# A float32 encoder block on one core: side work re-laned, operand parts made earlier, more weight halves kept

## The chip, the cores and the metric

The kernel runs on one NeuronCore of a Trainium2 chip. The metric is the device time of one execution in microseconds; the core's five engines (TensorE or PE, VectorE or DVE, ScalarE or ACT, GpSimd or POOL, SyncE or SP) run their own instruction streams in order and meet through semaphores. GpSimd does almost nothing here. Nearly all DMAs are issued from SP's queue, a few from ScalarE's.

## The reference

One layer (DEPTH is 1) on x of 2048 frames by 1024 channels, float32:

```
h = rmsnorm(x); proj = h @ w_in            # 1024 -> 512 | 2*512 | 1024 | 1024
u_pool, u_glu, g_a, g_b = split(proj)
A = pool_mixer(u_pool)      # 4 groups of 128: trailing mean over 2/4/8/16 frames minus self,
                            # times pool_w[g], times pool_scale, then @ w_pool_out (512 -> 1024)
B = conformer_conv(u_glu)   # a*sigmoid(gate); causal depthwise conv, 31 taps; layernorm; silu;
                            # then @ w_conv_out (512 -> 1024)
merged = sigmoid(g_a) * A + sigmoid(g_b) * B
x = x + rmsnorm(merged @ w_o)              # 1024 -> 1024
h = rmsnorm(x)
x = x + rmsnorm(square(relu(h @ w_up)) @ w_down)   # 1024 -> 4096 -> 1024
```

## The kernel before

Arithmetic. Every float32 operand is split into a high and a low part (`split`, L194; `split_w` for weights, L201): ScalarE casts the high part, VectorE subtracts it from the source to get the low one, and a product is three matmuls (high by high, high by low, low by high). On top of that the big projections use a scheme of seven block products in place of eight: an `Octet` (L365) runs products 1 to 7 on sums and differences of weight blocks (`weight_parts`, L258) and of token blocks (`token_parts`, L318). One product is 24 matmuls of 128x512. Operands are tiles of 128 x 1024.

Blocks and stages. The 2048 frames are two blocks of 1024. For each block: input projection (1 pool octet, 2 GLU octets, 2 octets for each gate: 49 products), branch A (`branch_a`, L901, 8 products), merge with branch B (`merge`, L922, 8 products), output projection (`out_proj`, L948, 8 products of 48 matmuls), up-projection (`mlp_up`, L1029, 8 octets, 56 products). The order on TensorE is: input 0, A 0, input 1, B 0, wo 0, A 1, up 0, B 1, wo 1, up 1, then the down-projection of both blocks in four slabs of 28 products (`down_product`, L1345), the last slab block by block, with the last norm behind it. Intermediate tensors (gates, convolution results `yd`, normed results `zd`, pooled results `mxd`, hidden activations `fd`) go through DRAM.

Side work. Convolution (`conv_steps`, L724: 31 VectorE operations per group of 128 channels, line 746), the layer norm and silu behind it (`norm_steps`, L761) and the pooling (`pool_steps`, L822, with four small products "mix") are generators. A `Lane` (L1074) advances its generators by a rate, and `bg` (L1103) calls every lane once after each product; `yield n` makes a lane sit out n calls. `behind` (L146) ties what they issue behind the instructions already issued for the main line, so that each engine's order is set when the program is built; `high_priority(offset=...)` moves what is issued within it that many instructions ahead. Weight loads and splits stand 260 ahead (`AHEAD`), 45 in the first stage.

In block 1's input projection one lane holds the rest of block 0's convolution, then `norm_steps(0, 1)`, then `pool_steps(1)`; what is left of it is issued after the last product by `empty` (L1112). Block 1's convolution runs in lanes beside B 0, wo 0 (rate 6, stopped after six calls) and up 0 (1.2, then 2.5), its norm behind it in up 0.

Weights. In block 0 the low halves of the input projection's weights, and for some octets the block sums, are written to DRAM (`kept`, through `flush`, L310, one product later) and loaded again in block 1. `load_w` (L213, for A, B and wo) splits each weight anew at every use. `out_proj` of block 0 runs both halves of the tokens (t = 0 and 1) under one weight, and that of block 1 one half after the other.

Parts. `Parts` (L350) makes an operand pair per step: for up 0 in branch A of block 1 (three steps of the norm's chain, then five parts), for up 1 only when up 1 begins.

Pools, in tiles of 128 x 1024: raw weights `wr` 5, weight sums `ws` 2, high and low weight halves 3 each, `big` 28 for operands, `tr` 8 for passing results, PSUM 3 accumulators.

Of the kernel before, what the change touches and what calls it, by code (L numbers as in the profile page):

```python
# [15 lines left out]
P = 128  # L16
# [3 lines left out]
TB = 1024  # L20
# [45 lines left out]
def block_kernel(  # L66
# [22 lines left out]
    p_wr = pool("pwr", 5)  # L89
# [76 lines left out]
    mean_c = p_const.tile([P, P], F32R, tag="meanc", name="mean_c")  # L166
    nc.gpsimd.memset(f32(mean_c), 1.0 / CW)
# [88 lines left out]
    kept = {}  # L256

    def weight_parts(src, key, b, keep, raw):  # L258
# [15 lines left out]
        def source(i):  # L274
            if i in (1, 2, 4):
                return get({1: 0, 2: 1, 4: 3}[i])
            if (key, i, "sum") in kept and b:
                t = mk(p_wr, "wr")
                load(t, kept[key, i, "sum"])
                return t  # L280
# [27 lines left out]
    later, due = [], []  # L308

    def flush():  # L310

        while due:
            load(*due.pop())
        due.extend(later)
        later.clear()
# [34 lines left out]
    class Parts:  # L350
# [8 lines left out]

        def need(self, i):  # L360
# [4 lines left out]
    class Octet:  # L365
# [13 lines left out]
        def run(self, i, then, bg):  # L379
# [11 lines left out]
            elif i == 2:  # L391
                self.sink(0, 0, ps, self.s1)
# [12 lines left out]
    def run_octets(octets, bg):  # L405
# [3 lines left out]
        for n, (o, i) in enumerate(jobs):  # L409
            o.run(i, jobs[n + 1][1] if n + 1 < len(jobs) else None, bg)  # L410
# [127 lines left out]
    p_tr = pool("ptr", 8)  # L538
# [97 lines left out]
    def in_stats(b):  # L636

        r = mk(p_ss, "r")
        for t in (0, 1):
# [13 lines left out]
            yield from inv_rms_steps([ss], inv_d, TR, 3, got)  # L653
# [70 lines left out]
    def conv_steps(b, groups):  # L724
# [8 lines left out]
        for c in groups:  # L733
# [5 lines left out]
            for k in range(TAPS):  # L739
# [9 lines left out]
                if k == 15 and c != groups[-1]:  # L749
                    nv = get(c + 1)  # L750
# [10 lines left out]
    def norm_steps(b, lag):  # L761
# [3 lines left out]
        mu = mk(p_y, "y")  # L765
        y = {}

        def prefetch(c):
            y[c] = window()
            load(y[c], yd[b, c, 0])  # L770

        for t in (0, 1):
            s = slice(t * T, (t + 1) * T)
            rb = mk(ps_rb, "rb", F32, (P, T))
            nc.tensor.matmul(rb, mean_c, sh[:, s], start=True, stop=False)
            nc.tensor.matmul(rb, mean_c, sl[:, s], start=False, stop=True)
            nc.scalar.copy(mu[:, s], rb)
            prefetch(t)
        yield 1
        ss = mk(p_ss, "sm")  # L780
        sq = {}
        for c in range(CC):
            sub(y[c], y[c], mu)
            load(yd[b, c, 0], y[c])
            sq[c] = ss if c == 0 else tr()
            nc.scalar.activation(sq[c], y[c], AF.Square)
            if c + 2 < CC:
                prefetch(c + 2)
            if c > 1:
                add(ss, ss, sq[c - 1])  # L790
            yield 1
        add(ss, ss, sq[CC - 1])
        yield lag
        r = mk(p_ss, "r")
        halves = [ss[:, t * T : (t + 1) * T] for t in (0, 1)]

        def got(t, rb):
            nc.scalar.copy(r[:, t * T : (t + 1) * T], rb)
            prefetch(t)

        yield from inv_rms_steps(halves, inv_c, TR, lag, got)
        yield 1
        hl = {}
        for c in range(CC + 1):
            if c < CC:
                mul(y[c], y[c], r)
                sg, ln = tr(), tr()
                nc.scalar.activation(sg, y[c], AF.Sigmoid, scale=col(C_LG + c), bias=col(C_LB + c))
                nc.scalar.activation(ln, y[c], AF.Identity, scale=col(C_LG + c), bias=col(C_LB + c))
                if c + 2 < CC:  # L810
                    prefetch(c + 2)
            if c:
                for i, part in enumerate(hl):
                    load(zd[b, c - 1, i], f32(part))
                yield
            if c < CC:
                yield 1
                mul(ln, ln, sg)
                hl = split(ln, *TR)
                yield  # L820

    def pool_steps(b):  # L822

        pw = []
# [9 lines left out]
        for g in range(CC):  # L834
            w, m = WINDOWS[g], 1
            while m < w:
                lo = HALO - (w - 2 * m)
                s2 = window(W)
# [13 lines left out]
            if not pw:  # L852
# [720 lines left out]
```

## Time and profile before

| what | value |
|---|---|
| median of 3 runs | 2504.81 us (2504.07 to 2507.45) |
| the profiled execution | 2504.89 us, of which its span is 2503.1 us |
| PE busy | 2254.7 us (90% of the span) |
| DVE busy | 1724.4 us (69%) |
| ACT busy | 1025.4 us (41%) |
| DMA | 538.93 MB, mean 215 GB/s |
| mean granted TensorE clock | 0.946 |

Busy time is the time in which an engine has an instruction in work; for matmuls, which are pipelined, a busy engine can still run at a lower granted clock, and the profile lists that clock by stretch. In rows of groups or of a timeline, the name ahead of the arrow is what is written, the names behind it what is read, `x` the count; in brackets stands the idle time before the first of them and what released it. In rows by stretch the columns are length, busy time and count of each engine, granted clock, busy share of the DMA engines, and GB/s.

### The profile page before, as it was taken

What the parts mean: (1) busy time and instruction counts of PE and PEld (TensorE: products, weight loads), DVE (VectorE), ACT (ScalarE), POOL (GpSimd) and SP (SyncE); (2) the same over time, 40 slices, a digit from 0 to 9 for tenths busy, and PEclk for the clock granted to TensorE, in tenths of its full rate; (3) what the DMA queues carried; (4) which work ended last, traced back from release to release, by engine and by line L of the source; (5) the groups of instructions that cost most, each with busy time, mean ns of one, the idle gap of its engine ahead of it and who ended that gap; (6) DMA issues with size and microseconds to landing.
All of it is one profiled execution on the core that took longest, in us unless ns stands there. A gap on an engine that the chain in (4) does not pass through costs nothing.

```text
span 2503.1 us, 24957 instructions
## 1 busy us (share of the span) xinstructions
PE 2254.7 (90%) x9600; PEld 1832.9 (73%) x9600; DVE 1724.4 (69%) x1685; ACT 1025.4 (41%) x1066; POOL 1.1 (0%) x11
## 2 busy tenths in 40 slices
PE   6898999999779987999869878999899999999885
PEld 5687877788667765888747656888678888787663
DVE  6797778883477497998653686767534566559676
ACT  5333443335422244445523464555344322223452
POOL 0000000000000000000000000000000000000000
PEclk9999999999889998999979888999899999999896
DMA  5667997657981562335583445786655454546774
GB/s 189 243 235 252 338 372 260 228 208 285 341 330 59 201 222 82 135 140 179 201 295 101 162 150 189 256 299 255 231 180 187 168 193 176 177 160 235 269 269 159
DMA packets 151320, 538.93 MB, mean 215 GB/s; under 512 B 17825, under 2 KB 17953, under 8 KB 151201
## 3 DMA queue, kind: packets, MB, share of 16 engines
q1 hardware_dynamic: 138528, 491.20, 55.0%
q10 hardware_dynamic: 12672, 46.14, 4.8%
q8 instruction: 75, 1.23, 0.2%
q14 instruction: 45, 0.36, 0.0%
HBM read 359.45 MB, written 177.83 MB: 215 GB/s over the span
## 4 chain that ended last, share of the span: by engine, by line
PE 79%; DVE 9%; DMA 6%; ACT 2%; issue 2%; SPq 1%; DVEq 0%; ACTq 0%
PE up L228 23%; PE down L228 23%; PE wo L228 7%; PE glu L228 6%; PE ga L228 6%; PE gb L228 4%; PE A L228 4%; PE B L228 3%; PE pool L228 2%; DMA tr<-fd 2%; DVE tr L119 2%; DVE y L746 1%; DVE tr L116 1%; DVE big L119 1%; DVE wl L119 1%
## 5 line engine op out<-in xcount | busy, mean ns | idle before, releaser
L228 PE MATMUL up<-big,wh 128*128 128x512 f32 x1792 | 497.8, 399 | 60.1 <-DVE tr L116 21.0
L228 PEld LDWEIGHTS up<-big,wh 128*128 128x128 f32 x1792 | 343.9, 193 | 140.8 <-ACT big L197 39.6
L228 PE MATMUL down<-fo,wh 128*128 128x512 f32 x896 | 359.1, 401 | 31.0 <-ACT fo L1340 31.0
L228 PE MATMUL down<-tr,wh 128*128 128x512 f32 x896 | 359.3, 401 | 15.3 <-DVE tr L119 15.3
L204 ACT CAST wh<-wr 128x1024 fp32r<-128x1024 f32 x170 | 177.8, 1048 | 473.7 <-PE up L228 106.6
L746 DVE SCALAR_TENSOR_TENSOR y<-v,cst,y 128x1024 f32<-128x1024 f32 x240 | 307.7, 1282 | 4.9
L228 PE MATMUL down<-fo,wl 128*128 128x512 f32 x896 | 284.1, 399 | 0.0
L228 PE MATMUL up<-big,wl 128*128 128x512 f32 x896 | 282.2, 397 | 0.0
L204 ACT CAST wh<-ws 128x1024 fp32r<-128x1024 f32 x124 | 130.6, 1053 | 323.9 <-PE up L228 138.8
L119 DVE TENSOR_TENSOR wl<-wr,wh 128x1024 fp32r<-128x1024 f32 x129 | 156.3, 1212 | 111.5 <-ACT wh L204 110.3
L228 PEld LDWEIGHTS down<-fo,wh 128*128 128x128 f32 x896 | 173.5, 194 | 73.7 <-ACT fo L1340 37.6
L228 PEld LDWEIGHTS down<-tr,wh 128*128 128x128 f32 x896 | 173.4, 194 | 58.9 <-DVE tr L119 22.9
L228 PEld LDWEIGHTS down<-fo,wl 128*128 128x128 f32 x896 | 173.1, 193 | 36.2
L228 PEld LDWEIGHTS up<-big,wl 128*128 128x128 f32 x896 | 172.7, 193 | 36.7
L1340 ACT CAST fo<-tr 128x1024 fp32r<-128x1024 f32 x112 | 117.5, 1050 | 197.1 <-DMA tr<-fd 104.9
L119 DVE TENSOR_TENSOR tr<-tr,fo 128x1024 fp32r<-128x1024 f32 x112 | 136.8, 1222 | 82.7 <-ACT fo L1340 82.7
L116 DVE TENSOR_TENSOR big<-big,down 128x1024 f32<-128x1024 f32 x88 | 107.1, 1219 | 125.6 <-PE down L228 122.7
L119 DVE TENSOR_TENSOR wl<-ws,wh 128x1024 fp32r<-128x1024 f32 x116 | 141.5, 1220 | 67.7 <-ACT wh L204 67.6
L228 PE MATMUL glu<-big,wh 128*128 128x512 f32 x448 | 126.1, 402 | 21.2 <-DVE big L119 11.7
L228 PE MATMUL wo<-big,wh 128*128 128x512 f32 x512 | 129.1, 393 | 7.2 <-ACT big L197 6.0
L228 PE MATMUL gb<-big,wh 128*128 128x512 f32 x448 | 124.3, 400 | 8.0 <-ACT wh L204 8.0
L228 PE MATMUL ga<-big,wh 128*128 128x512 f32 x448 | 121.4, 393 | 6.3 <-ACT wh L204 6.3
(147 smaller groups left out, 3075.4 us busy)
## 6 DMA issues: line engine op xcount, KB each, us to landing
tr<-fd SPq DMA_DIRECT2D x134, 512.0 KB, 5.3
wr<-w_up SPq DMA_DIRECT2D x68, 512.0 KB, 3.9
wr<-w_down SPq DMA_DIRECT2D x66, 512.0 KB, 4.1
fd<-tr ACTq DMA_DIRECT2D x56, 512.0 KB, 2.8
wr<-w_in SPq DMA_DIRECT2D x53, 512.0 KB, 5.4
kept<-wl SPq DMA_DIRECT2D x49, 512.0 KB, 4.7
wl<-kept SPq DMA_DIRECT2D x49, 512.0 KB, 4.3
fd<-tr SPq DMA_DIRECT2D x48, 512.0 KB, 3.1
```

The lines of the kernel that those rows point to most:

```text
L116: return nc.vector.tensor_tensor(o, a, b, op=ALU.add)
L119: return nc.vector.tensor_tensor(o, a, b, op=ALU.subtract)
L204: nc.scalar.copy(hi[:, :n], src[:, :n])
L228: i = nc.tensor.matmul(ps, w[wp][:, (at + k) * P : (at + k + 1) * P], rhs[k][xp], start=start and n == 0, stop=stop and n == len(order) - ...
L746: nc.vector.scalar_tensor_tensor(acc, v[:, k : k + TB], wk, acc, op0=ALU.mult, op1=ALU.add)
L1340: nc.scalar.copy(hi, t)
```

## The change

1. Block 1's input projection: the convolution's rest and the norm of block 0 form one lane (rate 3.8); once the pool octet is done, `pool_steps(1)` starts in a second lane (rate 2), and `conv_steps(1)` in a third that stays idle until both are done. Block 1's convolution then runs at 0.5 beside B 0, 2 beside wo 0, and 1.2, then 2.8, in up 0.
2. Output projection: both blocks run one token half after the other; once the first half's root is spread, each of the last two products of the second half is followed by two steps of operand parts (`made`). The pooled tiles for branch A of block 1 are loaded at (2, 1), not after the last product. `merge` goes through t = 0 first.
3. `load_w` keeps low halves too: it stores them at the first use and loads them at the later ones.
4. `weight_parts`: loads stay at the larger offset, sums and splits stand 40 ahead. Product four of a stage is copied out of PSUM by ScalarE (`hold`).
5. `norm_steps` works in `tr` tiles with the reads one call ahead, and each group takes a call of its own.
6. Down: the first five products' cells lie in `big` tiles and the first are loaded one product earlier; block 0's last two up octets also store the two differences that block 1 stores; the block sums are joined in slab two through lanes, for both blocks, and `bg` is called after every product.
7. Pools: `wr` 4, `tr` 9; the pooling's weight is split once; the constant for the mean goes, its factor moves into the copy; DMA scratch 256 for 1024.

```diff
-    p_wr = pool("pwr", 5)
+    p_wr = pool("pwr", 4)
...
-    def load_w(src, n=TB):
+    def load_w(src, key):
         with tc.high_priority(offset=ahead[0]):
             raw = mk(p_wr, "wr")
-            load(raw[:, :n], src)
-            return split_w(raw, n)
+            load(raw, src)
+            known = kept.get((key, "low"))
+            w = split_w(raw, low=known)
+        if known is None:
+            kept[key, "low"] = dram("kept")
+            later.append((kept[key, "low"], f32(w[1])))
+        return w
...
         def part(i):
             with tc.high_priority(offset=ahead[0]):
+                for q in {1: (0,), 2: (1,), 4: (3,), 7: (0, 2), 5: (2, 3), 6: (2, 3, 0), 3: (1,)}[i]:
+                    if (key, i, "sum") not in kept or not b:
+                        get(q)
+                if (key, i, "sum") in kept and b:
+                    source(i)
+            with tc.high_priority(offset=40):
                 t = source(i)
                 w = split_w(t, low=kept[key, i, "low"] if keep and b else None)
...
+        def some(self, raw, n):
+            self.raw = raw
+            for _ in range(n):
+                self.step()
...
             elif i == 2:
-                self.sink(0, 0, ps, self.s1)
+                self.sink(0, 0, self.held(ps) if hold else ps, self.s1)
...
-            o.run(i, jobs[n + 1][1] if n + 1 < len(jobs) else None, bg)
+            o.run(i, jobs[n + 1][1] if n + 1 < len(jobs) else None, bg, n == 3)
...
-    p_tr = pool("ptr", 8)
+    p_tr = pool("ptr", 9)
...
-        keys = [(c, t) for c in range(CPS) for t in (1, 0)]
+        keys = [(c, t) for c in range(CPS) for t in (0, 1)]
...
+                    if (c, t) == (2, 1):
+                        early()
                     if chain is not None:
                         with behind():
-                            next(chain, None)
-            if ts == halves[-1]:
-                early()
+                            if next(chain, 0) == 0 and c >= 2:
+                                made(raw, 2)
...
+            late = b or u >= 2 * SLABS - 2
...
-                if b and (m, t) == (1, 0):
+                if late and (m, t) == (1, 0):
                     h = tr()
                     sub(h, o, f["e"])
                     keep("t4", h)
...
-    lanes += [Lane(3.3, *rest, norm_steps(0, 1), pool_steps(1))]
+    done = set()
+
+    def marked(gen, k):
+        yield from gen
+        done.add(k)
+
+    def behind_all(gen, *ks):
+        while not done.issuperset(ks):
+            yield 1
+        yield from gen
+
+    rest = [marked(chain_of(*rest), "conv")]
+    lanes += [Lane(3.8, *rest, marked(norm_steps(0, 1), "norm"))]
+
+    def pooling():
+        lanes.append(Lane(2, marked(pool_steps(1, False), "pool")))
+        lanes.append(Lane(2.0, behind_all(conv_steps(1, (0, 1, 2, 3)), "conv", "pool")))
...
+    conv1 = lanes.pop()
     empty()
-    lanes += [Lane(1, conv_steps(1, (0, 1, 2, 3)))]
+    conv1.rate = 0.5
+    lanes.append(conv1)
     merged = merge(0, bg)
...
-    conv1.rate = 6
...
-    chain, raw = out_proj(0, merged, ((0, 1),), paced, lambda: fetched.extend(fetch_spread(mxd, 1)))
+    conv1.rate = 2
+    parts = Parts(lambda ops: token_parts(ops, lambda c, t: parts.raw(c, t), *BIG, TR))
+    chain = out_proj(
+        0, merged, ((0,), (1,)), bg, parts.some, lambda: fetched.extend(fetch_spread(mxd, 1))
+    )
...
     def faster():
-        conv1.rate = 2.5
+        conv1.rate = 2.8
...
-        if b and m is not None:
+        if (b or s == LAST) and m is not None:
             a, m = {4: "t4", 5: "t1"}[i], None
...
-    then(lambda: got.append(token_cells(*jobs[0])), octs[-1], 7)
+    then(lambda: got.append(token_cells(*jobs[0], BIG)), octs[-1], 5)
...
-                lanes += [Lane(2, recombine(1)), Lane(2, fin[0, 1].steps(2), fin[0, 0].steps(2))]
+                lanes += [Lane(2, fin[0, 1].steps(2), fin[0, 0].steps(2))]
...
-        if (s, i, b) == (LAST - 1, DOWN[-1], 0):
-            drain(recombine(0))
+        if s == LAST - 1 and i == 1:
+            lanes.append(Lane(1, recombine(b, ((2, 1), (1, 6), (7, 1), (1, 5), (3, 1)))))
+        if s == LAST - 1 and i == 7:
+            lanes.append(Lane(1, recombine(b, ((4, 7), (5, 7)))))
+        if (s, i, b) == (LAST - 1, DOWN[-1], 1):
+            empty()
```

More of the change, by code (lines that the diff above doesn't have):

```diff
@@ L946, in block_kernel, with out_proj, make @@
     q2 = {}
-    def out_proj(b, merged, halves, bg, early=none):
+    def out_proj(b, merged, halves, bg, made, early=none):
         o, x, rbs = {}, {}, {}
         chain = None
+        def make(c, t):
+            mul(two(o[c, t]), two(o[c, t]), per_token(rbs[t]))
+            add(x[c, t], x[c, t], o[c, t])
+            load(x1d[b, c, t], x[c, t])
+            gained(o[c, t], x[c, t], C_MPRE, c)
+            return o[c, t]
+        raw = lazily(make)
         for ts in halves:
@@ L1196, in step @@
             parts.step()
+    parts.need(2)
     branch_a(1, mixed, step)
```

185 lines of the change are left out of this document (89 added, 96 removed).

## The prediction

> **What bounds the kernel now.** I read the page first (busy times, the chain that ended last), then busy time by stage, then TensorE's waits and the rows at each of them.
>
> ```profile
> span 2503.1 us, 24957 instructions
> PE 2254.7 (90%) x9600; PEld 1832.9 (73%) x9600; DVE 1724.4 (69%) x1685; ACT 1025.4 (41%) x1066; POOL 1.1 (0%) x11
> ...
> PE 79%; DVE 9%; DMA 6%; ACT 2%; issue 2%; SPq 1%; DVEq 0%; ACTq 0%
> ```
>
> TensorE is idle for 2503.1 - 2254.7 = 248.4 us. The chain is TensorE for 79%. What a product costs when nothing is in the way is in one row of the chain, and what a pause costs beside its idle time in two rows of TensorE's timeline:
>
> ```profile
> 387.65 10.88 PE pool L228 x48
> ```
> ```profile
> 173.16 1.52 PE L228 MATMUL ga<-big,wh 128*128 128x512 f32 x6
> 221.89 2.92 PE L228 MATMUL ga<-big,wh 128*128 128x512 f32 x6 [6.33 <-ACT wh L204]
> ...
> 929.46 2.90 PE L228 MATMUL up<-big,wh 128*128 128x512 f32 x6 [6.93 <-DVE tr L116]
> 1460.30 2.90 PE L228 MATMUL up<-big,wh 128*128 128x512 f32 x6 [9.36 <-DVE tr L116]
> ```
>
> 48 matmuls in 10.88 us: 5.44 us for a product of 24, the floor below. After a pause of 6 to 9 us six matmuls take 2.9 us, not 1.52: a pause costs 1.4 us and more at a lower clock, beside its idle time. So I count a stage's loss as its length less the floor of its products.
>
> ```profile
> core 0: us, PE busy (x) PEld busy (x) DVE busy (x) ACT busy (x) POOL busy (x), PEclk, DMA share, GB/s
> 0.00:170.40 170.40, 139.37 (x580) 113.50 (x581) 124.88 (x134) 75.02 (x80) 1.12 (x11) 0.98 0.64 224
> 170.40:259.50 89.10, 82.77 (x360) 68.09 (x360) 70.67 (x77) 36.05 (x37) 0.00 (x0) 0.96 0.70 257
> 259.50:344.10 84.60, 82.23 (x359) 67.64 (x359) 59.28 (x67) 35.38 (x37) 0.00 (x0) 0.98 0.93 349
> ...
> 387.60:444.80 57.20, 51.25 (x223) 40.90 (x221) 50.78 (x44) 23.32 (x24) 0.00 (x0) 1.00 0.76 264
> 444.80:589.40 144.60, 143.28 (x624) 118.20 (x625) 115.30 (x94) 53.17 (x54) 0.00 (x0) 0.99 0.67 234
> 589.40:708.90 119.50, 93.26 (x382) 74.03 (x382) 54.47 (x62) 51.34 (x52) 0.00 (x0) 0.86 0.85 319
> 708.90:761.00 52.10, 47.72 (x204) 38.67 (x203) 43.86 (x39) 14.11 (x14) 0.00 (x0) 0.96 0.70 259
> 761.00:847.40 86.40, 86.27 (x371) 70.99 (x371) 57.61 (x48) 22.45 (x29) 0.00 (x0) 0.98 0.18 57
> 847.40:900.80 53.40, 50.18 (x214) 40.34 (x214) 32.98 (x46) 14.78 (x19) 0.00 (x0) 0.94 0.89 337
> 900.80:1242.80 342.00, 317.91 (x1368) 258.96 (x1367) 291.21 (x264) 168.12 (x171) 0.00 (x0) 0.96 0.41 146
> 1242.80:1327.80 85.00, 51.57 (x206) 39.77 (x206) 48.04 (x41) 28.60 (x27) 0.00 (x0) 0.80 0.74 266
> 1327.80:1415.30 87.50, 87.45 (x381) 71.94 (x381) 37.05 (x45) 35.44 (x45) 0.00 (x0) 0.98 0.38 132
> 1415.30:1776.30 361.00, 324.99 (x1386) 265.63 (x1387) 256.70 (x257) 192.83 (x196) 0.00 (x0) 0.93 0.64 229
> 1776.30:2264.00 487.70, 469.23 (x2015) 383.41 (x2014) 270.06 (x229) 160.67 (x159) 0.00 (x0) 0.98 0.50 177
> 2264.00:2366.00 102.00, 86.36 (x355) 68.75 (x353) 81.22 (x87) 40.59 (x43) 0.00 (x0) 0.92 0.73 264
> 2366.00:2473.00 107.00, 92.64 (x375) 72.21 (x375) 74.07 (x98) 49.95 (x58) 0.00 (x0) 0.90 0.68 243
> ```
>
> The stages: block 0's input projection to 344.1; branch A of block 0 and block 1's input projection to 708.9; merge (B) and output projection (wo) of block 0 to 847.4; branch A of block 1; up-projection of block 0 (56 products) to 1242.8; B and wo of block 1; up of block 1 to 1776.3; down. No engine is full in the stages that lose most (589.4: DVE 54 of 119.5 us, DMA 0.85; 1242.8: DVE 48 of 85): they wait for chains of latencies. The changed kernel issues the same 9476 matmuls, so the whole question is idle time and clock.
>
> **The change, stage by stage.** The sum is made against the profiled execution, 2504.9 us (2503.1 of span and 1.8 around it), which is also the median shown (2504.81).
>
> Start to 344.1. Copying the fourth product's accumulator out first ("hold") frees its PSUM buffer without waiting for VectorE's add: of the wait of 2.54 us there I take 1.5 off. The 6.33 us at 221.9 are a weight load queued behind a store:
>
> ```profile
> SPq L125 <- DVE y L746: 8.7, 1, 8.7
> ```
>
> In the built order the weights of those products stand ahead of that store: 6.33 and 1.4 of clock less. Against it one raw buffer less (five to four), 0 to 6 us by the same row; I take 7 off, bounds 0 and 9.
>
> 344.1 to 847.4. 8 + 49 + 8 products and wo (16 product equivalents), with four small mixes of 1.36: 446 us; the stage has 503, loss 57. Where 38 go is seen in the chain:
>
> ```profile
> 627.31 6.82 DMA v<-yd
> 657.88 12.15 PE gb L228 x42
> 679.25 7.21 DMA v<-ud
> 690.27 6.25 DMA v<-ud
> ```
>
> Block 1's pooling stands behind block 0's convolution and norm in one lane, and is emptied out after the last product. In two lanes all four of its mixes come before the last gate's products. The price is VectorE's: 31 taps more stand ahead of B. A tap and a plain operation, back to back:
>
> ```profile
> 444.66 14.48 DVE L746 SCALAR_TENSOR_TENSOR y<-v,cst,y 128x1024 f32<-128x1024 f32 x11
> 1423.50 4.62 DVE L119 TENSOR_TENSOR big<-big,big 128x1024 fp32r<-128x1024 f32 x4
> ```
>
> 1.32 and 1.155 us. Between the third mix's result and the fourth mix's operand the built order has 16 taps and 14 plain operations, 37.2 us, against six products, 32.6: TensorE waits about 5 at the fourth mix, with latencies 8, and the gate products queued behind the mix wait with it. The 8 us lost before 444.8 are VectorE's too and stay. Behind that, the last gate's 17 products (92.5 us) have 74 transfers of 512 KB queued beside them, 38.8 MB. At 349 GB/s, which the row at 259.5 reached with DMA 0.93 busy, that is 111 us, 19 over; spread over the merge behind it, I take 14 for both (bounds 0 and 19). The Trainium skill (DMA: Bandwidth & Descriptors, "Where 436 GB/s comes from") puts the HBM side at about 358 GB/s per core; by it the stretch is 108 us, 16 over, and the sum 2 us higher; the row scaled to full DMA is 375 GB/s, above the page's figure, so the row decides. With 3 for wo (its weights now loaded once per half) the loss is 33, not 57, less 3 because t = 0 is merged first and wo starts on it: 27 off, bounds 10 and 40.
>
> Branch A of block 1, 53.4 for 43.5. The pooled tiles are fetched two products earlier, but the last one is queued behind a weight buffer that comes free with wo's end, and the gate loads behind the fourth weight: 1 off, bounds -5 and 6.
>
> Up of block 0: 342 for 304.6, loss 37. Before, five steps of splitting precede it, one operand pair after the other being awaited (6.93 above is one of a dozen waits). Now four splits are made inside wo and five steps beside branch A. From the last branch A result to the operands of the eighth product the built order has 7 taps and 24 plain operations, 37 us, against 38 of products; the tenth then waits 3. Loss 10: 27 off, bounds 12 and 32.
>
> B of block 1: 85 for 43.5, loss 41.5. The norm ends after the last up product:
>
> ```profile
> 1255.25 5.46 DMA v<-yd
> 1274.15 5.78 DMA big<-zd
> ```
>
> Eleven taps fewer are left for up (70 for 81) and the lane runs at 2.8, not 2.5; counting its calls, conv ends at call 34 of 56 and the norm's 19 calls at 53. In the built order the last z is split before the result of the sixth product from the end, 27 us ahead. Loss 4: 37 off, bounds 15 and 41. wo behind it has two more loads per product (kept low halves): 2 on.
>
> Up of block 1: 361 for 304.6, loss 56. Two operand pairs are now made inside wo, weight sums no longer hold up VectorE (they are computed 40, not 260, instructions ahead; their loads stay at 260), and "hold" frees the accumulator of the wait of 9.36. The second half's root chain stays: 21 plain operations (24 us), 18 small ones and two trips to TensorE before the fifth product, against 21.8 us of products. I take half of the losses before 1545 away: 18 off, bounds 5 and 30.
>
> Down, three slabs: 488 for 457. First cells loaded earlier into free tiles; recombination spread over slab two, whose VectorE is 55% busy: 10 off, bounds 0 and 15. The last slab, block 0: 102 for 76. Recombination leaves it and two of its cells come as one load each, not two and a subtraction:
>
> ```profile
> L116 DVE TENSOR_TENSOR big<-big,big 128x1024 f32<-128x1024 f32 x40 | 47.8, 1218 | 0.1
> ```
> ```profile
> ACT fo L1340 <- DMA tr<-fd: 31.8, 14, 4.9
> ```
>
> Block 1's 14 of those 40 additions (17 us) go; the casts that TensorE waits for themselves wait for cells to land, and the second cell load moves one product ahead: 16 off, bounds 5 and 24. Block 1's half and the tail are queued as before: 0. Stores added in up (low halves, two more combinations) and 55 DMA issues on SP lie beside products with DMA 0.41 to 0.64 busy: 0; where DMA is full they are in the 38.8 MB.
>
> Sum: 1.5 + 7 + 27 + 1 + 27 + 37 - 2 + 18 + 10 + 16 = 142.5 off: 2362 us. The bounds add up to 40 and 197.
>
> The clock is the other thing to weigh. The sum takes it from the windows: of the 142.5 about 95 are listed waits and 47 the lower clock after them. The Trainium skill (TensorE: Matmul & The Clock Gate, "Part 1: The HAM clock gate") has the clock at half until some 3.4 us of work have passed. That makes 1.7 us for each of some 25 pauses removed, an estimate from the page of 43, and a sum of 2366. The rows' 2.9 for 1.52 agree.
>
> **Rivals.** One: half of it is handed back. Block 1's background loads share SP's one queue with the weights; if they wait there as 627.31 and 657.88 show, the stage to 847.4 gains nothing (27 back), the norm of block 1 ends late by half (18), and up starts on waits still (17): 2362 + 62 = 2424. For it: DMA 0.85 busy there before anything is packed closer. Against: DMA at 0.41 and TensorE-paced queues in up.
>
> Two, slower: weights arrive late everywhere. Of 210 products of the octets, each cast (1.05 us) and subtraction stands at 40 instructions' lead, little more than one product. It decides from 142.5 / 210 = 0.68 us per product; a wait of one cast and one subtraction (2.2 us) would give 2362 + 460. Against: in the built order all but 5 casts stand at least three products ahead (all but 7 before).
>
> Three: the waits only move, as latencies of the same chains: 2500 to 2510. For it: VectorE keeps 1672 of its 1685 instructions. Against: at 589.4 and 1242.8 it works less than 60%.
>
> Four: the bounds' good side, 2300.
>
> **Chances.** Forecast 0.62 (2320 to 2405), one 0.27 (to 2490), two 0.05, three 0.03 (0.02 of it within 0.2%, about what a measurement can tell from no change), four 0.03. Faster 0.92, same 0.02, slower 0.06. The range runs from 2315, most of case four left out, to 2440, which holds the nearer half of case one.
>
> **What would show it.** Right: no wait for big<-zd ahead of B of block 1; all mixes of block 1 before its last gate is done, with DMA over 0.9 in that gate; no wait over 5 us in the first ten products of block 0's up; a shorter first half of the last slab. Wrong: waits on wh or wl in the middle of up or of the gates; a wait at the fourth mix far above 8 us; B of block 1 still over 60 us.

## The result, and the profile after

The changed kernel takes 2411.39 us in the median of 4 runs (2408.20 to 2417.28), the kernel before 2505.19 beside it (2504.07 to 2507.45): a ratio of 0.9627, 95% interval 0.9606 to 0.9648. The forecast was 2362 us with a range from 2315 to 2440. The sign and the range held; of the 142.5 us forecast, 93.8 came. The time lies outside the 2320 to 2405 that the forecast called its own case, and inside the stretch that it gave to its first rival. The profiled execution took 2413.18 us, 2411.4 of them span.

The page of the changed kernel, its busy times and the chain that ended last:

```profile
PE 2234.3 (93%) x9600; PEld 1824.6 (76%) x9600; DVE 1688.1 (70%) x1672; ACT 1036.1 (43%) x1077; POOL 1.0 (0%) x10
...
PE 72%; DVE 15%; DMA 6%; issue 4%; ACT 3%; SPq 0%; DVEq 0%; ACTq 0%
```

TensorE's idle time fell from 248.4 to 2411.4 - 2234.3 = 177.1 us. In the chain VectorE has 15% where it had 9%: the time that is left is more VectorE's than before. Busy time by stage of the changed kernel (the columns are those explained for the kernel before):

```profile
326.80:379.10 52.30, 46.20 (x194) 37.42 (x193) 30.37 (x27) 21.12 (x28) 0.00 (x0) 0.93 0.91 339
379.10:524.50 145.40, 127.26 (x518) 101.95 (x517) 123.43 (x103) 48.23 (x49) 0.00 (x0) 0.93 0.68 232
524.50:632.30 107.80, 89.26 (x370) 72.37 (x369) 83.93 (x77) 37.27 (x39) 0.00 (x0) 0.89 0.72 254
632.30:719.60 87.30, 80.95 (x341) 65.99 (x340) 59.06 (x61) 42.33 (x43) 0.00 (x0) 0.96 0.90 326
719.60:763.10 43.50, 43.50 (x193) 36.04 (x192) 33.88 (x29) 11.69 (x12) 0.00 (x0) 1.00 0.94 344
763.10:851.70 88.60, 88.60 (x396) 73.39 (x395) 54.30 (x59) 39.73 (x50) 0.00 (x0) 1.00 0.70 238
851.70:911.50 59.80, 52.71 (x203) 41.98 (x202) 31.83 (x42) 15.18 (x18) 0.00 (x0) 0.86 0.78 291
911.50:1248.60 337.10, 314.86 (x1370) 257.68 (x1369) 274.73 (x251) 174.58 (x174) 0.00 (x0) 0.98 0.47 174
1248.60:1292.10 43.50, 43.50 (x193) 36.02 (x192) 27.08 (x23) 12.36 (x12) 0.00 (x0) 1.00 0.93 349
...
1725.80:2191.30 465.50, 459.82 (x2017) 379.09 (x2017) 289.32 (x247) 156.42 (x155) 0.00 (x0) 1.00 0.50 184
2191.30:2273.10 81.80, 78.90 (x348) 64.20 (x347) 48.35 (x57) 38.05 (x40) 0.00 (x0) 1.00 0.83 286
2273.10:2381.40 108.30, 92.31 (x381) 71.86 (x380) 76.69 (x99) 52.03 (x60) 0.00 (x0) 0.92 0.69 254
```

Four stages now run at or near their floor with a clock of 1.00: B and wo of block 0 (719.6 and 763.1), B of block 1 (1248.6, where 78.9 us had gone), and the first three down slabs. Three take longer than before: branch A of block 0 (52.3 us for 43.5), block 1's projection (340.5 for 318.2) and branch A of block 1 (59.8 for 50.2). Up of block 0 has a new wait of 9.26 us near its end. Up of block 1 and the last slab's second half still lose most against their floors, some 40 and 32 us. Laid against the terms of the forecast, from the first matmul of each stage in both traces:

| stage | before, us | after, us | off | forecast off |
|---|---|---|---|---|
| start to block 1's first product | 387.5 | 379.1 | 8.4 | 8.5 |
| block 1's input projection, B 0, wo 0 | 462.9 | 472.6 | -9.7 | 27 |
| branch A of block 1 | 50.2 | 59.8 | -9.6 | 1 |
| up of block 0 | 342.2 | 337.1 | 5.1 | 27 |
| wait for z and B of block 1 | 78.9 | 43.5 | 35.4 | 37 |
| wo and up of block 1 | 454.6 | 433.7 | 20.9 | 16 |
| down, slabs 0 to 2 | 488.7 | 465.5 | 23.2 | 10 |
| last slab, block 0 | 97.3 | 81.8 | 15.5 | 16 |
| the rest | 140.8 | 138.3 | 2.5 | 0 |

The last column adds up to the 142.5, the one before it to the difference of the spans, 91.7. (The last three rows divide the down matmuls by count, so their bounds lie a few us from those of the forecast's table.) Three rows are missing 69 us; two others give 18 more than was forecast. The first two rows are not the forecast's own terms: it ended its first term where branch A of block 0 begins (344.0 us before, 326.8 after) and counted that branch in the second. By its own bounds the start gained 17.1 us, not 8.5, and the second term lost 18.4, where 27 off was forecast. TensorE's waits over 3 us from branch A of block 0 to the end of up of block 0:

```profile
334.68 0.80 PE L240 MATMUL A<-big,wh 128*128 128x512 f32 x1 [5.66 <-DMA big<-mxd]
386.03 1.65 PE L240 MATMUL pool<-big,wl 128*128 128x512 f32 x3 [5.45 <-DMA wl<-kept]
476.41 2.93 PE L240 MATMUL glu<-big,wh 128*128 128x512 f32 x6 [5.38 <-DVE tr L116]
587.34 1.22 PE L790 MATMUL rb<-tr,ones 128*128 128x512 f32 x2 [12.32 <-ACT tr L195]
620.52 2.93 PE L240 MATMUL ga<-big,wh 128*128 128x512 f32 x6 [5.88 <-DVE tr L116]
676.23 0.96 PE L240 MATMUL gb<-big,wl 128*128 128x512 f32 x3 [3.39 <-DMA wl<-kept]
880.02 0.80 PE L240 MATMUL A<-big,wh 128*128 128x512 f32 x1 [3.55 <-DVE tr L122]
1219.05 2.93 PE L240 MATMUL up<-big,wh 128*128 128x512 f32 x6 [9.26 <-ACT tr L390]
```

None of them stands at the fourth mix, where 8 us were forecast. There are three questions: what holds TensorE at 587, what slows branch A of block 1, and what the 9.26 us at the end of up are. The wait at 334.68, in branch A of block 0, is for pooled tiles: the fourth mix of that pooling stands at 319.95, only 7 us ahead of the branch, where it stood 33 us ahead (311.13) before. Every run below has this wait (4.7 to 6.9 us) and takes 52 to 55 us there; none was made to test it.

### The profile page after: what moved, and what is told of

The parts are those of the page before. It is cut to its first block, busy times and chain, and to the rows that moved or that the text cites. A ratio compares the mean times of both kernels' runs of the same rounds, so it can differ in the third digit from the quotient of the medians.

```text
span 2411.4 us, 25045 instructions
## 1 busy us (share of the span) xinstructions
PE 2234.3 (93%) x9600; PEld 1824.6 (76%) x9600; DVE 1688.1 (70%) x1672; ACT 1036.1 (43%) x1077; POOL 1.0 (0%) x10
## 4 chain that ended last, share of the span: by engine, by line
PE 72%; DVE 15%; DMA 6%; issue 4%; ACT 3%; SPq 0%; DVEq 0%; ACTq 0%
PE down L240 23%; PE up L240 17%; PE wo L240 7%; PE gb L240 5%; DVE y L760 4%; PE ga L240 4%; PE B L240 4%; PE glu L240 4%; PE A L240 4%; PE pool L240 3%; DVE tr L119 2%; DVE tr L116 2%; DMA tr<-yd 2%; DMA wr<-w_in 1%; DVE wl L119 1%
## 5 line engine op out<-in xcount | busy, mean ns | idle before, releaser
L202 ACT CAST wh<-wr 128x1024 fp32r<-128x1024 f32 x176 | 185.0, 1051 | 467.4 <-issue 80.5
L240 PE MATMUL down<-tr,wh 128*128 128x512 f32 x896 | 353.6, 395 | 13.0 <-DVE tr L119 13.0
L240 PE MATMUL down<-fo,wh 128*128 128x512 f32 x896 | 352.9, 394 | 9.6 <-ACT fo L1383 9.5
L240 PE MATMUL down<-fo,wl 128*128 128x512 f32 x896 | 278.9, 393 | 0.0
L1383 ACT CAST fo<-tr 128x1024 fp32r<-128x1024 f32 x102 | 107.0, 1050 | 188.0 <-DMA tr<-fd 128.3
L119 DVE TENSOR_TENSOR tr<-tr,fo 128x1024 fp32r<-128x1024 f32 x102 | 124.6, 1221 | 72.9 <-ACT fo L1383 72.7
L119 DVE TENSOR_TENSOR wl<-wr,wh 128x1024 fp32r<-128x1024 f32 x103 | 125.5, 1218 | 46.5 <-ACT wh L202 45.9
L116 DVE TENSOR_TENSOR tr<-tr,tr 128x1024 f32<-128x1024 f32 x65 | 79.4, 1221 | 66.6 <-ACT tr L536 57.9
```

The source lines that it names most:

```text
L116: return nc.vector.tensor_tensor(o, a, b, op=ALU.add)
L119: return nc.vector.tensor_tensor(o, a, b, op=ALU.subtract)
L202: nc.scalar.copy(hi[:, :n], src[:, :n])
L240: i = nc.tensor.matmul(ps, w[wp][:, (at + k) * P : (at + k + 1) * P], rhs[k][xp], start=start and n == 0, stop=stop and n == len(order) - ...
L1383: nc.scalar.copy(hi, t)
```

## Experiments

Each run starts from the changed kernel. Its time is to be read beside 2411; the intervals of the ratios are some 0.2% wide to each side, so 5 us between two runs say nothing. Among the runs that leave a stage alone its length repeats within 2 to 4 us (up of block 0 takes 337.1 to 338.8, block 1's first gate 104.5 to 107.8); only branch A of block 1 is looser, 53.4 to 60.8 us.

### The wait at 587: VectorE's taps, or transfers

First, VectorE's load alone: every second tap of two groups is not issued.

```
-                else:
+                elif b or c < 2 or k % 2 == 0:
                     nc.vector.scalar_tensor_tensor(
```

> The changed kernel with every second convolution tap of block 0's groups 2 and 3 left out (30 taps of 1.32 us, about 40 us of VectorE beside block 1's input projection; the output is not the reference's). Nothing else moves: steps, loads, stores and matmuls stay. Theory V (VectorE's taps hold back block 1's input projection: the 12.32 us of the norm's mean and the 5.88 behind it): the stretch from block 1's first product to the start of B, 340.5 us in the changed kernel, falls by 15 to 30 us and the time to 2380 to 2397. Rival D (transfers and their queue hold it back): VectorE is free sooner and waits for the same landings; the stretch stays within 6 us and the time at 2405 to 2412.

2392.46 us (ratio to before 0.9549, 0.9528 to 0.9571). From block 1's first product to B: 323.4 us for 340.5; both waits of the gate (12.32 and 5.88) give way to one of 3.80, and what follows from B on is together as long as before within 3 us. Theory V holds, D falls for this place. But 40 us less on VectorE brought 17.

Second, TensorE's part alone: the matmuls of the mean three products later.

```
         sh, sl = split(sums[b], *TR)
-        yield 3
+        yield 3 if b else 6
```

> The changed kernel with six products instead of three between block 0's split of the convolution sums and the matmuls of their mean. Theory V: those matmuls stand in TensorE's order before VectorE has the sums; three products later (16 us) they are ready: the wait of 12.32 us goes, the norm behind it ends up to 16 us later but B has slack for part of it: 5 to 12 us off, 2399 to 2406. Rival N (the norm itself is on the path to B): the wait moves to B's z or to the last gate: 2409 to 2420.

2415.45 us (0.9637, 0.9623 to 0.9651): no gain, theory V falls, and the time is where rival N had it. TensorE's timeline of this run:

```profile
589.28 2.92 PE L240 MATMUL ga<-big,wh 128*128 128x512 f32 x6 [14.48 <-ACT tr L390]
720.19 0.80 PE L240 MATMUL B<-big,wh 128*128 128x512 f32 x1 [5.32 <-DMA big<-zd]
```

The mean is out of the way, and TensorE waits at the same place, 14.48 us, for a copy on ScalarE (L390) that frees a PSUM accumulator; the later norm then costs B 12 us (55.7 for 43.5), the row at 720.19 the longest of its waits. So the matmuls of the mean were not the cause. What ScalarE and VectorE did there in the changed kernel stands in their timelines:

```profile
586.24 1.04 ACT L195 CAST tr<-sm 128x1024 fp32r<-128x1024 f32 x1 [7.71 <-DVE sm L116]
587.19 1.02 ACT L729 ACTIVATE tr<-ga 128x1024 f32<-128x1024 f32 x1
588.11 1.03 ACT L195 CAST tr<-tr 128x1024 fp32r<-128x1024 f32 x1
588.24 0.33 ACTq L129 DMA_DIRECT2D sad<-tr  x1
589.04 1.01 ACT L390 COPY tr<-ga 128x1024 f32<-128x1024 f32 x1
```

```profile
579.71 5.24 DVE L760 SCALAR_TENSOR_TENSOR y<-v,cst,y 128x1024 f32<-128x1024 f32 x4
584.98 1.23 DVE L116 TENSOR_TENSOR sm<-sm,y 128x1024 f32<-128x1024 f32 x1
```

VectorE has worked with one pause of 0.52 us since 520 and reaches the sum of the convolution (`sm`) at 584.98. ScalarE's next instruction is the cast of that sum; it waits 7.71 us for it, and behind it stand a sigmoid and the copy at 589.04 that TensorE needs. Every octet makes three such copies, in the kernel before too. The Trainium skill (PSUM — Partial Sum Buffer, "Engine vs sequencer instructions") says that ScalarE's and VectorE's queues are strictly first in, first out; the rows agree, no ScalarE work passes the cast. If that is the cause, the cast has to be issued later:

```
+        if not b:
+            yield 4
         sh, sl = split(sums[b], *TR)
```

> The changed kernel with block 0's split of the convolution sums (its cast on ScalarE and its subtraction on VectorE) issued four products later, the matmuls of the mean three after it as before. Theory H (it is ScalarE's place in line: the cast waits for VectorE's sums, and the copy that frees TensorE's PSUM buffer stands behind it): the wait of 12 to 14 us near 587 falls below 4 us, and since the norm ends later only a part is lost at B: 6 to 12 us off, 2399 to 2405. Theory B (VectorE is full from 523 to 585 and TensorE must wait for it anyway): the wait moves to the split operands of the next product, within 5 us of 2411.

2402.42 us (0.9584, 0.9568 to 0.96). The waits of 12.32 and 5.88 us are gone, no other over 3 us takes their place between 480 and 620, and the gate that took 107.8 us takes 81.3. B then waits for z, though:

```profile
703.80 0.80 PE L240 MATMUL B<-big,wh 128*128 128x512 f32 x1 [4.43 <-DMA big<-zd]
```

B takes 56.0 us for 43.5 and the second gate 91.0 for 87.3, so that 9 us remain of 26. Theory H holds with the price that it named.

### The reads and the lanes

```
-            if c + 1 < CC:
-                prefetch(c + 1)
+            if not b and c + 2 < CC:
+                prefetch(c + 2)
             sub(y[c], y[c], mu)
...
+            if b and c + 2 < CC:
+                prefetch(c + 2)
```

> The changed kernel with the norm's reads of the convolution rows asked for two steps ahead again (block 0: first pass; block 1: both passes, through the window buffers), not one. Theory R (VectorE, in order, stands 6 to 9 us in front of each late read, and TensorE behind it: 9.26 us at 1219 and part of 5.88 at 620): both waits go below 3 us, 10 to 16 us off: 2395 to 2402. Rival D (the one queue is the limit; earlier reads only push the weights back): new waits on weight tiles, 2407 to 2414.

2408.89 us (0.9615, 0.9591 to 0.9639). The wait at the end of up stays (9.86 us at 1217), and so does that of the mean (12.45); in place of the one at 620 stands one of 3.13 for a weight. Reads that land late aren't what the two large waits hang on.

The wait at the end of up has the same form as the one at 587. In the changed kernel ScalarE and VectorE do this ahead of it:

```profile
1214.58 1.24 ACT L823 ACTIVATE tr<-tr,cst 128x1024 f32<-128x1024 f32 x1 [2.98 <-DVE tr L122]
...
1217.98 1.01 ACT L390 COPY tr<-up 128x1024 f32<-128x1024 f32 x1
```

```profile
1213.32 1.22 DVE L122 TENSOR_TENSOR tr<-tr,r 128x1024 f32<-128x1024 f32 x1 [3.30 <-DMA tr<-yd]
```

The norm's sigmoid waits for VectorE's multiplication, and the copy that frees TensorE's accumulator stands behind it. With the reads asked for sooner VectorE no longer waits for the row (`yd`), but the sigmoid still waits 2.60 us for VectorE, which has other operations in front.

```
-    lanes += [Lane(3.8, *rest, marked(norm_steps(0, 1), "norm"))]
+    lanes += [Lane(3.3, *rest, norm_steps(0, 1), marked(pool_steps(1, True), "pool"))]
...
-        lanes.append(Lane(2, marked(pool_steps(1, False), "pool")))
```

> The changed kernel with block 0's norm and block 1's pooling in one lane at the old rate of 3.3 (convolution, norm, pooling), all else as changed. Theory V (the second lane's pooling and the higher rate are what delay VectorE's sums): the wait at the mean goes, the mixes stand late again as before the change, and the last gate loses about what it lost there: the stretch from block 1's first product to B takes 321 to 335 us where the changed kernel takes 340.5, time 2392 to 2408. Theory P (two lanes pay, as the prediction had it): 350 to 365 us in that stretch, time 2420 to 2438.

2454.08 us (0.9795, 0.9781 to 0.981): 43 us slower, more than either theory had, and not where they looked. From block 1's first product to B and its output projection it takes 476.1 us, 3.5 more than with two lanes: the gate's wait is gone, the mixes' waits (10.78, 6.05 and 6.99 us) are back. The loss is at B of block 1:

```profile
1275.32 0.76 PE L240 MATMUL B<-big,wh 128*128 128x512 f32 x1 [21.30 <-DMA big<-zd]
```

Taps of the convolution (line 760) in up of block 0, in this run and then in the changed kernel:

```profile
913.20:1254.00 340.80, 130.39 (x102) 0.97 0.42 150
```
```profile
911.50:1248.60 337.10, 88.20 (x69) 0.98 0.47 174
```

With one lane the pooling ends late, block 1's convolution has 33 taps more left for up, and its norm isn't done when up is. What the second lane pays (together with the higher rate, which this run takes back as well), it pays 500 us further on: 36 of the 43 us are that wait and B. The wait of 5.38 us at 476 falls to 1.95 here, and block 1's first stretch (379 to 524) takes 138.4 us for 145.4.

### Branch A of block 1

```
-            known = kept.get((key, "low"))
+            known = kept.get((key, "low")) if key[0] != "po" else None
```

> The changed kernel with the low halves of branch A's four weight tiles computed in both blocks, not kept: four stores and four loads of 512 KB fewer, four subtractions (4.6 us) more on VectorE. Theory Q (branch A of block 1, 59.8 us for a floor of 43.5, waits for transfers that stand in one queue with those loads): 50 to 55 us there, 2402 to 2407. Rival (it waits for block 1's last mixed tiles and for VectorE, whatever is loaded beside them): 57 to 61 us there, 2409 to 2415.

2389.45 us (0.953, 0.951 to 0.955): 22 us off from one part of the change taken back, more than theory Q gave it. Branch A by stretch, in this run:

```profile
844.30:889.20 44.90, 44.90 (x203) 37.30 (x202) 34.07 (x44) 15.19 (x18) 0.00 (x0) 1.00 0.83 314
```

TensorE doesn't pause in it, at 314 GB/s for 291. SP's queue in the changed kernel, and the one long wait in it from 855 to 875:

```profile
851.85 0.32 SPq L125 DMA_DIRECT2D wl<-kept  x1
...
855.23 4.33 SPq L125 DMA_DIRECT2D big<-xt  x3
871.07 0.33 SPq L125 DMA_DIRECT2D wl<-kept  x1
871.44 0.43 SPq L125 DMA_DIRECT2D big<-xt  x1
871.91 0.90 SPq L125 DMA_DIRECT2D tr<-sad  x2
```
```profile
SPq L125 <- PE A L240: 11.4, 1, 11.4
```

and in the run without the kept halves:

```profile
842.66 2.22 SPq L125 DMA_DIRECT2D big<-xt  x4
844.97 1.55 SPq L125 DMA_DIRECT2D tr<-sad  x2
```

With kept halves a load of 512 KB has to wait for a free `wl` buffer, until a matmul of branch A has read it, and it waits in the queue: from 859.56 to 871.07 SP issues nothing, and the gate's loads (`tr<-sad`), which need no such buffer, stand behind it. Branch A's product waits for the gate's multiplication (3.55 us at 880), and before that 2.03 and 1.17 us for the last pooled tile, which is queued behind the load at 851.85; the rest of the loss is busy time at a lower clock (52.7 us busy at 0.86, where this run has 44.9 at 1.00). A subtraction on VectorE needs the same buffer, but it blocks no queue of transfers. The other 6 us are at block 1's first product, where stores and loads of the same kind precede the weights: 5.45 us at 386 become 1.60. Branch A of block 0 doesn't change (53.0 us), so its loss is not theirs.

The other low halves that the change keeps, those of B and the output projection, taken back as well:

```
-            known = kept.get((key, "low"))
+            known = None
```

> The changed kernel with the low halves of branch A's, branch B's and the output projection's weights computed in both blocks, none of the three kept (the projection and gate lows stay kept): 16 stores and some 24 loads of 512 KB fewer. Theory Q (kept lows cost where transfers fill the queue, in branch A of both blocks, and save nothing elsewhere): as without branch A's alone, 2384 to 2394, with B and the output projections of both blocks within 3 us of the changed kernel's. Rival (in B and the output projection they spare VectorE the subtractions that TensorE would wait for): 5 to 15 us above the run without branch A's alone, 2394 to 2405.

2391.06 us (0.9549, 0.9523 to 0.9575), the same as without branch A's alone. B and wo of both blocks take as long with them as without them (43.5 and 88.5 us): they save nothing there, and cost nothing.

### Operand parts made inside the output projection

```
-    chain = out_proj(1, merged, ((0,), (1,)), none, parts.some)
+    chain = out_proj(1, merged, ((0,), (1,)), none, lambda r, n: parts.some(r, 0))
```

and the same for block 0.

> The changed kernel without the operand parts made inside the output projections: they are made from branch A on (block 0) and from up's first product on (block 1), as before the change; all else as changed. Theory M (the parts made early are what removed the waits at the start of both up-projections): waits of 3 to 7 us come back in the first ten products of up of block 0, which takes 352 to 362 us for 337.1, and up of block 1 5 to 12 more: 2430 to 2450. Rival (those waits went for another reason, fewer taps and the hold, or moved into branch A): 2408 to 2420.

2413.69 us (0.963, 0.9607 to 0.9654): theory M falls. Up of block 0 keeps waits at its start like those of the changed kernel (1.82, 2.69, 1.53 and 2.00 us in this run); at up of block 1, there are two more waits, of 3.97 and 3.76 us, and wo and up together take 4.3 us more. What took the larger waits at the start of block 0's up away is thus something else that the run keeps. It may be the halves in turn, whose first root is ready inside the output projection, or the pair that is made ahead of branch A; neither was tried alone.

### The end of the up-projection, and down

```
-            late = b or u >= 2 * SLABS - 2
+            late = b
...
-        if (b or s == LAST) and m is not None:
+        if b and m is not None:
```

> The changed kernel with block 0's cells of the last slab made as before the change: two loads and a subtraction for two of its seven products, and without the three extra combinations that its last two up octets then needn't compute and store. Theory L (those extra subtractions are what lets VectorE fall behind at the end of up of block 0, 9.26 us at 1219): that wait falls below 4 us, 5 to 7 us back in up, and the last slab's first half loses 8 to 15: 2412 to 2420 in all. Rival (the wait is the norm's late rows alone, whatever up computes beside them): the wait stays at 8 to 10, and down loses as much: 2418 to 2428.

2408.89 us (0.9613, 0.9595 to 0.9631). The wait at the end of up falls from 9.26 to 6.90, the last slab's first half rises from 81.8 to 86.2: a small part of either theory's, and no difference in the sum that is clear of noise.

```
-        if s == LAST - 1 and i == 1:
-            lanes.append(Lane(1, recombine(b, ((2, 1), (1, 6), (7, 1), (1, 5), (3, 1)))))
-        if s == LAST - 1 and i == 7:
-            lanes.append(Lane(1, recombine(b, ((4, 7), (5, 7)))))
...
+        if (s, i, b) == (LAST - 1, DOWN[-1], 0):
+            drain(recombine(0, PAIRS))
```

and block 1's additions in a lane of the last slab.

> The changed kernel with the down accumulators joined as before the change: block 0's 14 additions at once behind its last product of slab two, block 1's 14 in a lane beside the last slab's first half. Theory J (the prediction's: joining in the last slab costs what it takes of VectorE there): slab two's end loses 5 to 10 us and the last slab's first half about 10: 2423 to 2432. Rival (the down-projection's 41 us come from the cells that are loaded whole): 2410 to 2417.

2422.24 us (0.9652, 0.9623 to 0.968). Slabs 0 to 2 are as long as in the changed kernel (465.4 us), the last slab's first half isn't:

```profile
2187.40:2282.20 94.80, 84.59 (x347) 68.14 (x346) 72.72 (x79) 38.74 (x42) 0.00 (x0) 0.93 0.70 250
```

94.8 us for 81.8, with 79 VectorE instructions for 57. Theory J holds in the last slab; in slab two, where it had 5 to 10 us, the additions cost nothing wherever they stand.

### Put together

Without branch A's low halves, with the split two products later, and with the convolution sooner:

```
-    conv1.rate = 0.5
+    conv1.rate = 1
...
-    conv1.rate = 2
+    conv1.rate = 3
```

> The changed kernel with three edits: branch A's low halves not kept, block 0's split of the convolution sums two products later, and block 1's convolution at 1 step per product beside branch B and 3 beside the output projection (0.5 and 2 in the changed kernel), so that some 20 taps (26 us of VectorE) leave up of block 0. If the first two add up: 2411 - 22 - 9 = 2380. Theory L (VectorE's load in up's end sets the 9.26 us): with the norm done some seven products sooner that wait goes as well, 2368 to 2374, and B and the output projection of block 0 stay within 3 us. Rival (VectorE is full beside the output projection too): waits of 5 to 15 us there instead, 2380 to 2392.

2374.72 us (0.948, 0.9457 to 0.9503), just above theory L's 2374 and below the rival's 2380. Up of block 0, all work and then the taps alone:

```profile
888.80:1208.10 319.30, 310.96 (x1370) 256.40 (x1368) 260.88 (x239) 173.98 (x174) 0.00 (x0) 0.99 0.50 182
```
```profile
888.80:1208.10 319.30, 75.72 (x59) 0.99 0.50 182
```

319.3 us for 337.1, with ten taps fewer (not the twenty expected): no wait over 1.2 us is left after the start. The runs with the first two edits keep that wait (8.96 us without the low halves, 8.54 with the later split), so the sooner convolution removed it: the norm's last split now ends some 50 us ahead of up's end, where it was 26. Whether the fewer taps or the norm's place did it, this run doesn't tell apart; the last octets' own additions are a smaller part (9.26 to 6.90 above). From block 1's first product to branch A the stretch is 466.7 us, and 466.2 in the low-halves run, so two products' delay of the split brought no gain here. What the gate gained (88.9 us for 107.8), the second gate (98.9) and B (52.3 for 43.5) lost again; the convolution's higher rate beside B, in the same run, may have its share in that.

The last run has the four products' delay, the mean two behind it, and for the second gate only low halves, no weight sums:

```
-        gate(1, parts, 5, sbd, "gb", "sums"),
+        gate(1, parts, 5, sbd, "gb", "lows"),
```

> The changed kernel with four edits: branch A's low halves not kept; block 1's convolution sooner (1 step per product beside branch B, 3 beside the output projection); block 0's split of the convolution sums four products later and its mean two behind that; and of the second gate only low halves kept, no weight sums (6 loads of 512 KB fewer in block 1's last gate and 8 stores fewer in block 0's, 8 operations or 9 us more on VectorE). Theory T (where the split is moved, transfers hold that gate and B: 6 loads are 9 us at the 328 GB/s seen there): the last gate and B of block 1 lose at most 8 us together, 2352 to 2366. Rival V (VectorE's additional sums and the later norm cost as much): the wait at B stays at 8 to 12, 2366 to 2380.

2355.09 us (median of 5, 2352.84 to 2359.87; ratio 0.9401, 0.9388 to 0.9414), the fastest kernel of this study, 56 us below the changed one. B of block 0, and in the second row block 1's last gate ahead of it:

```profile
689.80:744.30 54.50, 48.17 (x193) 38.17 (x192) 38.08 (x33) 11.18 (x11) 0.00 (x0) 0.91 0.88 322
602.10:689.80 87.70, 83.04 (x358) 67.89 (x357) 74.59 (x80) 45.56 (x46) 0.00 (x0) 0.96 0.87 313
```

The gate's 14 products took 98.9 us in the run before, 87.7 here. The first gate takes 80.5 us for 88.9. That B, which theory T's text calls block 1's, still loses 11 us, two more than in the run before: the bound of 8 is missed there, though the time is met. As the last run changes the split and the loads at once, the share of each is read from the place alone.

## Why the prediction was right, and where it was not

The start, 8.5 forecast, 8.4 measured in the table: that agreement is luck. By the forecast's own bounds the start gained 17.1 us, beyond its bound of 9: besides the 6.33 us at 221.9, a second wait of 2.37 us for a cast weight is gone. Branch A of block 0, which the sum put at its floor, then gave back 8.8 us, for pooled tiles that came no sooner (5.66 us at 334.68), and the next stage's start cost 5.45 that no step had. Why that pooling's fourth mix stands later than before (319.95, not 311.13) is open.

Block 1's stretch, "27 off, bounds 10 and 40", is the step that failed: it took 9.7 us more. Its first half was right: all mixes were done before the last gate, the last gate and B ran at 326 and 344 GB/s, and their waits for transfers were 6.4 us, less than the 14 allowed. What was wrong is the sentence that TensorE "waits about 5 at the fourth mix". The taps and the plain operations were counted against the mix's operand alone. The instruction that the backlog reached first was the cast of the convolution's sum, on ScalarE, with the copy behind it that frees an accumulator. The step priced VectorE's delay for its direct consumer and did not ask what stands behind that consumer on its own engine. The half-tap run puts 17 us on the backlog; the later split frees 26 us of the gate and hands back 12 at B.

Branch A of block 1, "1 off, bounds -5 and 6": -9.6. The place was named, the fourth weight ahead of the gate's loads and a weight buffer that comes free late; the term was mis-sized. Without the kept halves the branch takes 45.0 us, 15 less (8 less than the shortest of the runs that keep them), where the bounds allowed a loss of 5. With the 6 at block 1's first product, keeping branch A's low halves cost 21 us.

Up of block 0, "Loss 10: 27 off, bounds 12 and 32": 5.1. The waits at its start went as forecast, from 21.1 us in the rows over 1.2 us to 8.2. The step that failed is the one on the norm's 19 calls ending at 53 of 56, counted under B's 37 as if up paid nothing. The calls came where they were forecast (the last split 26 us ahead of up's end, for 27), but among the last octets' own work, and up lost 13.0 us in waits for ScalarE's copies out of PSUM from 1139 on. Ten taps moved ahead brought 17.8 back.

B of block 1, 37 forecast, 35.4 measured, and for the reason given: no wait for z ahead of it, 69 taps for 80 in up. The one-lane run shows what it hangs on: the start of block 1's convolution beside the gates.

Wo and up of block 1: 16 forecast, 20.9 measured; the parts made inside wo account for 4.3. Slabs 0 to 2: 10 forecast with bounds to 15, 23.2 measured. In the kernel before, the slabs' first 45 us held four waits of 1 to 3.5 us for cells, with slow matmuls behind them, the first of them:

```profile
1780.88 0.51 PE L228 MATMUL down<-fo,wh 128*128 128x512 f32 x1 [3.48 <-ACT fo L1340]
```

The changed kernel has none over 1.2 us there. Which of the extra buffers and earlier loads did that was not tried, so that these 13 us above the forecast, which help the total into the range, are luck as far as is known. The last slab: 16 forecast, 15.5 measured, 13 of them from the additions' place by the run that moves them back, and 4.4 from the cells by the run that makes them as before.

Of the rivals, the first came nearest: it said 2424 and had the stretch to 847 gain nothing because loads stand in SP's queue. That queue was the cause of 21 us, in branch A and ahead of it; of that stretch's other loss the half-tap run puts 17 us on VectorE's backlog, and the rival's two other parts (the norm of block 1, up's start) didn't come. Rival two (weights late at 40 instructions' lead) had nothing for it: the changed kernel has no wait of TensorE on `wh` at all, and those on `wl` are for loads. (Two of these, 3.39 and 2.96 us, do stand in the last gate, where the prediction had waits on `wl` among the signs of being wrong.) Rival three (the waits only move) was true of block 1's projection and of up of block 0, not of the whole. Two figures of the forecast are off without bearing on it: both traces have 9600 matmuls, not 9476, and the good bounds add up to 195, not 197, once the 2 us for wo are taken off.

One thing is left open: of block 1's first stretch (379 to 524), which takes some 18 us longer than before with two mixes (2.7) moved in, the taps left out bring 1, the low halves 4 to 6.5 and one lane at the old rate 7; these may overlap, and the rest has no run that separates it.

## What to carry to other kernels

When side work on one engine falls behind, look for the first instruction of another engine that waits for it, and price everything that stands behind that one: a cast that is issued too soon stops a queue that the main line needs. A load that must wait for a buffer is better placed behind the loads that need none (not tried here); to compute the same tile locally may cost an engine a microsecond and still be cheaper than 512 KB in front of other transfers. Side work pays or costs where it ends, which may be hundreds of microseconds behind the place that was changed, so follow a moved step to the last consumer.

## What the hardware showed

A blocked issue queue cost far more than the bytes: the four low-half loads move 2.1 MB, 6 us at the 349 GB/s seen at 1248.6, and cost 8 to 15 us in branch A with the transfers only 0.78 busy. A pause is paid twice, by its idle time and by slow matmuls behind it: after waits of 5.38, 5.88 and 9.26 us six of them took 2.93 us, where undisturbed they take 1.52. For short pauses the length alone doesn't tell the price: after 1.82 us six took 1.65, after 1.87 us 2.51.

```profile
410.92 2.51 PE L240 MATMUL pool<-big,wh 128*128 128x512 f32 x6 [1.87 <-ACT tr L390]
...
935.25 1.65 PE L240 MATMUL up<-big,wh 128*128 128x512 f32 x6 [1.82 <-ACT tr L390]
```
